# Expert values with the activations as the stationary operand, values streamed in 512 columns, and the second layer norm along the free dimension

## The chip, the core and the metric

One core of a Trainium2 chip runs the whole layer as one program. The metric is the device time of one execution in microseconds (us); the runs shown are three executions and their median.

## The reference

One layer of an encoder: 256 tokens, model width 2048. Each half is a residual sum with a gated branch and a layer norm:

```python
h = x * (1.0 + sc1) + sh1
x = layer_norm(DEEPNORM_ALPHA * x + g1 * hybrid_mixer(h, ...), ln1_g, ln1_b)
h = x * (1.0 + sc2) + sh2
x = layer_norm(DEEPNORM_ALPHA * x + g2 * peer(h, w_query, sub_keys, expert_u, expert_v), ln2_g, ln2_b)
```

`sh1 .. g2` come from `silu(c) @ W_ada + b_ada` (adaLN). `peer` picks 16 of 128 x 128 experts per head and token by product keys, takes `gelu(u . h)` of each picked expert times its softmax gate, and sums the experts' value rows with these weights:

```python
act = gelu(einsum('tkd,td->tk', u_sel, xb))
return einsum('tk,tkd->td', act * gb, v_sel)
```

## The kernel before, in words

The kernel computes the expert part densely: gates and activations of all 16384 experts for all 256 tokens, as 128 "columns" (the second key, `e2`) of 128 experts each (the first key, on the partitions). Its stages are: the input projection and the mixer; the output projection and the first layer norm; P3, the queries and the product keys; P4, gates and activations of all experts; P5, the expert values and the second layer norm. This change touches the end of the first layer norm (the residual), P3 and P5.

Arithmetic of full precision is made of matmuls on a shorter type (`fp32r`). A weight `w` is split into `hi` (a copy by ScalarE, L77) and `lo` (the rest, by VectorE, L80); an activation likewise (`split`, L118 and L119). `mm3` (L90 to L92) then adds three products to a sum: hi x hi, hi x lo and lo x hi. Weights come through `wsplit`: a load of half a megabyte on SyncE's queue (L74) into one of three `raw` tiles, then the two parts into one of three `hi` and `lo` tiles each. A few products, the "whole" ones of the input projection (L100), the score products (L736) and the transposes, take plain fp32 operands.

P5 before (L851 to L933): the sums of 16 chunks of the model dimension by 256 tokens lie in all eight PSUM banks, two chunks to a bank. A chunk's sum is 128 model columns (partitions) by 256 tokens (free). So for each expert column and each of its two halves of 1024 model columns, eight chunks follow each other: the stationary operand is a 128x128 piece of the values (`hi` or `lo`), the moving operand the 256 tokens' activations `ah` or `al`. The banks are opened beforehand by eight matmuls with a tile of zeros (L869). `GA` holds gates times activations; `a_pair` (L860) splits two columns of it at a time. It is two tiles, of FIRST = 98 and 30 columns: where the first has been used, the parts of the LAST = 6 last value columns lie (`last_column`, L874), and the end goes through these six by output chunk (L905), so that a chunk's layer norm can begin while others still grow.

Beside the values, `ada_step` (L896) loads the last part of W_ada, 16 steps of two halves, multiplies it by silu(c) on every partition (L151) and so makes `gate2`, which lies with the model dimension on the partitions (`mod[:, 5]`).

The end: gate2 and the residual `ax` (read from DRAM, written there by `residual`, L681) are put to each chunk (L916); `Norm` sums over chunks and, with a matmul by ones, over partitions; then come mean, reciprocal deviation, gain and shift (L923 to L932), and eight stores (L933). The output lies as [partition, chunk, token], and the host puts it in order.

`residual` is a generator: P3 takes two of its 16 steps per head (`next(keep)`), between the copies of the queries and the score products. The framework's scheduler, not the source's order, fixes each engine's order of instructions; weight loads carry a high priority, so they run ahead as far as free tiles allow. SyncE executes its queue in order: a load that waits for a free tile holds all that stand behind it.

Of the kernel before, what the change touches and what calls it, by code (L numbers as in the profile page):

```python
# [7 lines left out]
F32 = mybir.dt.float32  # L8
# [32 lines left out]
def layer_kernel(ctx, tc, I, out, dbg=None):  # L41
# [14 lines left out]
    ax_d = dram.tile([ND, P, S], F32, name="ax_d")  # L56
# [4 lines left out]
    iota = const.tile([P, NE], F32, name="iota")      # 0 .. 127  # L61
# [4 lines left out]
    mod = const.tile([P, 6, ND], F32, name="mod")     # shift1, 1 + scale1, gate1, shift2, 1 + scale2, gate2  # L66
    lnp = const.tile([P, 4, ND], F32, name="lnp")     # gains and shifts of the layer norms

# [1 line left out]
    def wsplit(src, pool=stream, width=1024, ahead=600, after=None):  # L70
        """A tile of weights and its two exact parts."""
# [30 lines left out]
    def proj(pss, srcs, mh, ml, nk, pool=stream, ahead_pool=None, after=None, before_last=None, beside=None, start=0):  # L102
        """pss[i][col, t] = sum over nk chunks k of srcs[i][p, k, col] * m(k)[p, t]."""
# [19 lines left out]
    def log_tables():  # L123
        """The set of tables that has both ln and exp."""
# [14 lines left out]
    def rsqrt(r, v, t):  # L139
        """One Newton step on r, which is near v ** -0.5; t is scratch."""  # L140
# [25 lines left out]
    class Norm:  # L166
        """LayerNorm of rT[p, d, t] over (d, p), chunk by chunk; s is the mean of the first chunk."""
# [12 lines left out]
        def add(self, d):  # L180
# [7 lines left out]
            else:  # L188
# [3 lines left out]
                # eps comes in once, as a share of each partition  # L192
# [5 lines left out]
        def finish(self):  # L198
            """The mean over s, and the reciprocal deviation, on every partition."""
# [21 lines left out]
    ys = [[None, None] for _ in range(32)]             # the mixer's output, in two parts  # L221
# [5 lines left out]
    scb = prm.tile([P, D], F32, name="scb")           # 2 silu(c), on every partition  # L227
# [20 lines left out]
    # dt and its sums, by token  # L248
# [17 lines left out]
    # the first half of the mixer's input as it is, for the products that take no parts  # L266
# [35 lines left out]
    def ada_input(d):  # L302
        """The mixer's input of chunk d, in two parts."""
# [12 lines left out]
    def unit_b(q, u):  # L316
        """What chunks 4q .. 4q + 3 of d add to two of the sums in SBUF."""
# [40 lines left out]
    # halves of the SSD convolution's weights: silu(u) = (u/2) (1 + tanh(u/2))  # L358
# [491 lines left out]
    with ExitStack() as p5:  # L850
# [18 lines left out]
        for b in banks:  # L869
            clear(zero, b)  # L870
# [124 lines left out]
```

## Time and profile before

| | us |
|---|---|
| median of three runs | 2599.3 (2595.35 to 2599.39) |
| span of the profiled execution | 2599.8 |
| TensorE busy in it | 2477.0 (95%) |
| VectorE busy | 1888.4 (73%) |
| ScalarE busy | 1388.1 (53%) |
| the values' matmuls, first start to last | 1844.2 to 2579.9 |

The profiled execution shows no time of its own beside its span, which lies 0.5 us above the median. Busy time of matmuls is modelled: their records overlap, so a stage is better read by counting how many of them start in a stretch of time. "PE" is the engine's matmuls, "PEld" the loads of the stationary operand, which have records of their own. A matmul on plain fp32 operands has two records.

### The profile page before, as it was taken

What the parts mean: (1) busy time and instruction counts of PE and PEld (TensorE: products, weight loads), DVE (VectorE), ACT (ScalarE), POOL (GpSimd) and SP (SyncE); (2) the same over time, 40 slices, a digit from 0 to 9 for tenths busy, and PEclk for the clock granted to TensorE, in tenths of its full rate; (3) what the DMA queues carried; (4) which work ended last, traced back from release to release, by engine and by line L of the source; (5) the groups of instructions that cost most, each with busy time, mean ns of one, the idle gap of its engine ahead of it and who ended that gap; (6) DMA issues with size and microseconds to landing.
All of it is one profiled execution on the core that took longest, in us unless ns stands there. A gap on an engine that the chain in (4) does not pass through costs nothing.

```text
span 2599.8 us, 50429 instructions
## 1 busy us (share of the span) xinstructions
PE 2477.0 (95%) x20176; PEld 2424.5 (93%) x20176; DVE 1888.4 (73%) x3281; ACT 1388.1 (53%) x2504; POOL 0.9 (0%) x7
## 2 busy tenths in 40 slices
PE   5889999999999799999999999999999999999997
PEld 5889888889999799999999999999899999999997
DVE  8788899889886899898888755555675444446545
ACT  3435576656434544499999744444334444445442
POOL 0000000000000000000000000000000000000000
PEclk9999999999999899999999999999999999999998
DMA  9887867687887665356666666666787555556651
GB/s 356 299 299 237 269 200 258 207 273 266 276 292 232 212 208 171 112 179 193 193 195 191 203 210 212 207 211 211 262 300 262 187 187 187 186 187 237 200 186 61
DMA packets 179596, 572.92 MB, mean 220 GB/s; under 512 B 20193, under 2 KB 42913, under 8 KB 179105
## 3 DMA queue, kind: packets, MB, share of 16 engines
q1 hardware_dynamic: 179362, 569.71, 66.3%
q8 instruction: 158, 2.59, 0.4%
q14 instruction: 76, 0.62, 0.1%
HBM read 556.98 MB, written 12.66 MB: 219 GB/s over the span
## 4 chain that ended last, share of the span: by engine, by line
PE 67%; DMA 15%; DVE 12%; ACT 3%; issue 2%; SPq 0%; ACTq 0%; DVEq 0%
PE ps_u L90 9%; PE ps_u L92 9%; PE ps_u L91 9%; PE ps_v L92 8%; PE ps_v L91 7%; PE ps_v L90 7%; DVE lo L80 5%; DMA adaw<-in_w_ada_dram 4%; DMA rT<-in_w_ada_dram 3%; DMA raw<-in_w_in_dram 3%; DVE adaw L151 2%; ACT hi L77 2%; DMA raw<-in_w_inB_dram 2%; PE ps_in L90 2%; PE ps_in L92 2%
## 5 line engine op out<-in xcount | busy, mean ns | idle before, releaser
L80 DVE TENSOR_TENSOR lo<-raw,hi 128x1024 fp32r<-128x1024 f32 (+1 forms) x800 | 968.7, 1213 | 522.1 <-ACT hi L77 516.3
L77 ACT ACTIVATE hi<-raw 128x1024 fp32r<-128x1024 f32 (+1 forms) x800 | 838.5, 1050 | 925.4 <-PE ps_v L91 308.9
L90 PE MATMUL ps_u<-h2h,hi 128*128 128x256 f32 x2048 | 573.2, 280 | 0.0
L92 PE MATMUL ps_u<-h2h,lo 128*128 128x256 f32 x2048 | 572.0, 279 | 0.0
L91 PE MATMUL ps_u<-h2l,hi 128*128 128x256 f32 x2048 | 571.6, 279 | 0.0
L92 PE MATMUL ps_v<-ah,lo 128*128 128x256 f32 x1952 | 548.4, 281 | 6.9 <-DVE lo L80 6.7
L90 PE MATMUL ps_v<-ah,hi 128*128 128x256 f32 x1952 | 545.4, 279 | 0.0
L91 PE MATMUL ps_v<-al,hi 128*128 128x256 f32 x1952 | 545.0, 279 | 0.0
L92 PEld LDWEIGHTS ps_u<-h2h,lo 128*128 128x128 f32 x2048 | 384.8, 188 | 0.0
L90 PEld LDWEIGHTS ps_u<-h2h,hi 128*128 128x128 f32 x2048 | 384.2, 188 | 0.0
L91 PEld LDWEIGHTS ps_u<-h2l,hi 128*128 128x128 f32 x2048 | 383.8, 187 | 0.0
L92 PEld LDWEIGHTS ps_v<-ah,lo 128*128 128x128 f32 x1952 | 366.9, 188 | 9.5 <-DVE lo L80 9.3
L91 PEld LDWEIGHTS ps_v<-al,hi 128*128 128x128 f32 x1952 | 367.5, 188 | 0.1
L90 PEld LDWEIGHTS ps_v<-ah,hi 128*128 128x128 f32 x1952 | 365.7, 187 | 0.3 <-issue 0.3
L90 PE MATMUL ps_in<-h2h,hi 128*128 128x256 f32 x768 | 223.2, 291 | 3.0 <-DVE mod L158 1.7
L92 PE MATMUL ps_in<-h2h,lo 128*128 128x256 f32 x768 | 218.4, 284 | 2.0 <-DVE lo L80 2.0
L151 DVE SCALAR_TENSOR_TENSOR adaw<-adaw,scb 128x1024 f32<-128x1024 f32 x160 | 193.6, 1222 | 34.1 <-DMA adaw<-in_w_ada_dram 33.6
L91 PE MATMUL ps_in<-h2l,hi 128*128 128x256 f32 x768 | 218.2, 284 | 0.0
L803 ACT ACTIVATE o<-eq,gT 128x128 fp32r<-128x128 f32 x512 | 160.1, 385 | 0.0
L90 PEld LDWEIGHTS ps_in<-h2h,hi 128*128 128x128 f32 x768 | 146.5, 191 | 9.2 <-issue 3.8
L92 PE MATMUL ps_o<-y,lo 128*128 128x256 f32 x512 | 145.7, 285 | 7.2 <-DVE lo L80 7.2
L92 PEld LDWEIGHTS ps_in<-h2h,lo 128*128 128x128 f32 x768 | 146.7, 191 | 4.3 <-DVE lo L80 2.2
(269 smaller groups left out, 4080.8 us busy)
## 6 DMA issues: line engine op xcount, KB each, us to landing
raw<-in_expert_u_dram SPq DMA_DIRECT2D x256, 512.0 KB, 3.8
raw<-in_expert_v_dram SPq DMA_DIRECT2D x244, 512.0 KB, 4.3
adaw<-in_w_ada_dram SPq DMA_DIRECT2D x160, 512.0 KB, 5.9
raw<-in_w_in_dram SPq DMA_DIRECT2D x110, 512.0 KB, 4.9
raw<-in_w_out_dram SPq DMA_DIRECT2D x64, 512.0 KB, 4.8
raw<-in_w_query_dram SPq DMA_DIRECT2D x64, 512.0 KB, 3.8
raw<-in_w_inB_dram SPq DMA_DIRECT2D x44, 512.0 KB, 4.4
rT<-in_w_ada_dram SPq DMA_DIRECT2D x32, 512.0 KB, 5.6
```

The lines of the kernel that those rows point to most:

```text
L77: A.activation(hi, raw, AF.Copy)
L80: V.tensor_tensor(lo, raw, hi.bitcast(F32), op=ALU.subtract)
L90: T.matmul(ps, wh, mh, start=start, stop=False)
L91: T.matmul(ps, wh, ml, start=False, stop=False)
L92: T.matmul(ps, wl, mh, start=False, stop=stop)
L151: V.scalar_tensor_tensor(w, w, 0.5, scb[:, cs], op0=ALU.mult, op1=ALU.mult, accum_out=macc[:, half, part % 2, d:d + 1])
L803: A.activation(o2[:, k], eq[:, i, 1].bitcast(F32), AF.Copy, scale=gT[:, k, t0 + i:t0 + i + 1])
```

## The change

- **Values.** A sum is now 128 tokens (partitions) by 512 model columns (free), four banks for each of two token blocks. The stationary operand is a 128x128 piece of `ah` or `al`, the moving one 512 columns of the values' parts. For a half of an expert column, eight matmuls with `hi` (two column groups, two token blocks, `ah` and `al`) come ahead of four with `lo`. The first expert column opens the banks itself; the zeros go.
- **adaLN.** A step stands behind every sixth expert column, no longer every seventh. At column 100 the sums are closed, `gate2` is written to DRAM and read back along the free dimension on every partition (`g2b`).
- **Residual.** In P3 each of the 16 chunks is transposed on TensorE (two transposes into one of the score products' two PSUM tiles), copied by ScalarE and written to DRAM by tokens.
- **End.** Four last columns, not six, go by token block and 512 columns. The layer norm's sums are taken along the free dimension as accumulators of the residual sum (VectorE) and of a square (ScalarE), per token; the gain and shift rows are loaded on every partition. The output is stored as [token, model dimension].
- FIRST goes from 98 to 66, LAST from 6 to 4. All else in the diff is comments.

```diff
-FIRST = 98         # expert columns before those that the end takes
-LAST = 6           # expert columns that the end goes through by output chunk
+FIRST = 66
+LAST = 4
...
-    def residual():
+    def residual(ps, ident):
         for d in range(ND):
             r = rT[:, d]
             V.tensor_tensor(r, r, rs, op=ALU.mult)
             A.activation(r, r, AF.Identity, scale=g1a[:, 0, d:d + 1], bias=g1a[:, 1, d:d + 1])
-            nc.sync.dma_start(ax_d[d], r)
+            pt = ps.tile([P, 2, P], F32, name="ps_r", tag="pm")
+            for tb in range(2):
+                T.transpose(pt[:, tb], r[:, tb * P:(tb + 1) * P], ident)
+            A.activation(r, pt.rearrange("p b d -> p (b d)"), AF.Copy)
+            nc.sync.dma_start(ax_d[:, :, d * P:(d + 1) * P].rearrange("b t d -> t b d"),
+                              r.rearrange("p (b d) -> p b d", b=2))
             yield
...
-        banks = [pv.tile([P, 2, S], F32, name="ps_v", tag="pm") for _ in range(8)]
-        ln = Norm(wk, pv, rT)
+        banks = [[pv.tile([P, 512], F32, name="ps_v", tag="pm") for _ in range(4)] for _ in range(2)]
+        g2b = wk.tile([P, D], F32, name="g2b")
...
-        zero = wk.tile([P, 512], BF16, name="zero5")
-        V.memset(zero, 0.0)
-        for b in banks:
-            clear(zero, b)
+        def mm_v(tb, c, ah, al, vh, vl, lo, start, stop):
+            ts = slice(tb * P, (tb + 1) * P)
+            if not lo:
+                T.matmul(banks[tb][c], ah[:, ts], vh, start=start, stop=False)
+                T.matmul(banks[tb][c], al[:, ts], vh, start=False, stop=False)
+            else:
+                T.matmul(banks[tb][c], ah[:, ts], vl, start=False, stop=stop)
...
             for half in range(2):
-                wh, wl = wsplit(I["expert_v"][e2, half])
-                for i in range(8):
-                    n = half * 8 + i
-                    mm3(banks[n // 2][:, n % 2], wh[:, i], wl[:, i], ah[:, e2 % 2], al[:, e2 % 2], False, False)
-            if e2 % 7 == 6 and e2 < 112:
-                ada_step(scb5, raw5[:2], 5, e2 // 7)
+                wh, wl = (w.rearrange("p k c -> p (k c)") for w in wsplit(I["expert_v"][e2, half]))
+                for lo in range(2):
+                    for j in range(2):
+                        js = slice(j * 512, (j + 1) * 512)
+                        for tb in range(2):
+                            mm_v(tb, 2 * half + j, ah[:, e2 % 2], al[:, e2 % 2], wh[:, js], wl[:, js], lo, e2 == 0, False)
+            if e2 % 6 == 5 and e2 < 96:
+                ada_step(scb5, raw5[:2], 5, e2 // 6)
+            if e2 == 100:
+                ada_sum(5, slice(0, ND))
+                nc.sync.dma_start(g2_d.rearrange("d p -> p d"), mod[:, 5])
+                nc.sync.dma_start(g2b, bass.AP(tensor=g2_d.tensor, offset=g2_d.offset, ap=[[0, P], [1, D]]))
...
+        def finish(tb):
...
+                ax = stream.tile([P, 1024], F32, name="ax", tag="raw", bufs=3)[:, :512]
+                nc.sync.dma_start(ax, ax_d[tb, :, c * 512:(c + 1) * 512])
+                V.tensor_tensor(r, banks[tb][c], g2b[:, c * 512:(c + 1) * 512], op=ALU.mult)
+                V.scalar_tensor_tensor(r, r, 1.0, ax, op0=ALU.mult, op1=ALU.add, accum_out=s[:, c:c + 1])
...
+                A.activation(ax, r, AF.Square, bias=sh, accum_out=s[:, 4 + c:5 + c])
...
+            for c in range(4):
+                r = rows5[tb][c]
+                V.scalar_tensor_tensor(r, r, mean, lng[c], op0=ALU.subtract, op1=ALU.mult)
+                V.scalar_tensor_tensor(r, r, rs, lnb[c], op0=ALU.mult, op1=ALU.add)
+                nc.sync.dma_start(out[tb * P:(tb + 1) * P, c * 512:(c + 1) * 512], r)
...
+        for tb in range(2):
+            fin = finish(tb)
+            next(fin)
+            for c in range(4):
+                cs = slice(c * 512, (c + 1) * 512)
+                for i in range(LAST):
+                    ah, al = as_[i // 2]
+                    for lo in range(2):
+                        mm_v(tb, c, ah[:, i % 2], al[:, i % 2], vs[i][0][:, cs], vs[i][1][:, cs], lo, False, i == LAST - 1)
+                next(fin, None)
```

In the changed kernel the two operations of `finish` on a bank are L939 and L940, its scaling L959 and L960, the load of `ax` L938, the write and the read of gate2 L914 and L915, the transposes L690, the copies behind them L691, and the values' matmuls L878, L879 and L881; other lines move by one to eight (the value loads are L75, `lo` is L81, the score products L742).

How TensorE's order begins P5 before, behind the eight zeros (out<-in, the moving operand first in each pair of names):

```order
L90 MATMUL ps_v<-ah,hi 128x256
L91 MATMUL ps_v<-al,hi 128x256
L92 MATMUL ps_v<-ah,lo 128x256
L90 MATMUL ps_v<-ah,hi 128x256
L91 MATMUL ps_v<-al,hi 128x256
L92 MATMUL ps_v<-ah,lo 128x256
```

And now, from the first matmul of P5 on:

```order
L878 MATMUL ps_v<-hi,ah 128x512
L879 MATMUL ps_v<-hi,al 128x512
L878 MATMUL ps_v<-hi,ah 128x512
L879 MATMUL ps_v<-hi,al 128x512
L878 MATMUL ps_v<-hi,ah 128x512
L879 MATMUL ps_v<-hi,al 128x512
L878 MATMUL ps_v<-hi,ah 128x512
L879 MATMUL ps_v<-hi,al 128x512
L881 MATMUL ps_v<-lo,ah 128x512 x4
```

A half column is 12 matmuls instead of 24, and `lo` is wanted behind the eighth instead of at the third.

SyncE's queue where the last half of W_ada (L162, tile rT) is loaded before (L881 is a last value column):

```order
L162 DMA rT_23081<-in_w_ada_dram 128x1024
L74 DMA raw<-in_expert_v_dram 128x1024
L881 DMA rT_23081<-in_expert_v_dram 128x1024
L74 DMA raw<-in_expert_v_dram 128x1024
L881 DMA rT_23081<-in_expert_v_dram 128x1024
```

And now (L163 is W_ada, L893 a last value column, g_d gate2 in DRAM):

```order
L163 DMA big_23146<-in_w_ada_dram 128x1024
L75 DMA raw<-in_expert_v_dram 128x1024
L893 DMA big_23146<-in_expert_v_dram 128x1024
L75 DMA raw<-in_expert_v_dram 128x1024 x2
L914 DMA g_d<-mod 128x16x1
L893 DMA big_23146<-in_expert_v_dram 128x1024
L75 DMA raw<-in_expert_v_dram 128x1024 x2
L915 DMA g2b<-g_d 128x2048
L75 DMA raw<-in_expert_v_dram 128x1024 x2
```

The write of gate2 and its reading back stand between value loads, three of those behind the last half of W_ada. Ahead of that last half the queue had 42 value loads before, and has 48 now.

The end of SyncE's queue now:

```order
L75 DMA raw<-in_expert_v_dram 128x1024 x118
L938 DMA ax<-ax_d 128x512 x3
L926 DMA lnrow<-in_ln_dram 128x1024 x4
L938 DMA ax<-ax_d 128x512 x4
L961 DMA out_dram<-big_23146 128x512 x4
L938 DMA ax<-ax_d 128x512
L961 DMA out_dram<-big_23146 128x512 x4
```

The eighth load of the residual stands behind the four stores of token block 0.

## Rows read from the trace of the kernel before

**Rows 1.** The page: span, part 1 (TensorE) and the granted clock of part 2.
```profile
span 2599.8 us, 50429 instructions
PE 2477.0 (95%) x20176; PEld 2424.5 (93%) x20176; DVE 1888.4 (73%) x3281; ACT 1388.1 (53%) x2504; POOL 0.9 (0%) x7
PEclk9999999999999899999999999999999999999998
```

**Rows 2.** Stretches of P5, the values' instructions alone: length, busy (count), clock, DMA, GB/s.
```profile
1844.20:1968.20 124.00, 117.17 (x961) 114.67 (x960) 0.00 (x0) 0.99 0.88 299
1968.20:2550.00 581.80, 581.73 (x4938) 581.41 (x4937) 0.00 (x0) 1.00 0.58 193
2550.00:2580.30 30.30, 29.99 (x252) 29.58 (x250) 6.32 (x15) 1.00 0.21 62
```

**Rows 3.** The values' matmuls of L92 (L90 and L91 alike): ns min/median/max, starts.
```profile
L92 PE MATMUL ps_v<-ah,lo x1952: 276/280/415, 1845.0 to 2545.3; 128*128 128x256 f32 x196
L92 PE MATMUL ps_v<-ah,old x96: 278/279/280, 2545.6 to 2579.9; 128*128 128x256 f32 x96
```

**Rows 4.** One stretch of 100 us inside P5, all engines, TensorE first.
```profile
2200.00:2300.00 100.00, 100.00 (x851) 100.00 (x851) 48.34 (x44) 42.55 (x45) 0.00 (x0) 1.00 0.57 186
```

**Rows 5.** Timeline of TensorE at P5's start: start us, us, what.
```profile
1845.01 0.41 PE L92 MATMUL ps_v<-ah,lo 128*128 128x256 f32 x1
...
1846.50 0.41 PE L90 MATMUL ps_v<-ah,hi 128*128 128x256 f32 x1
```

**Rows 6.** Timeline and source view of the whole products, L100.
```profile
274.46 3.62 PE L100 MATMUL ps_in<-h2w,raw 128*128 128x256 f32 x16
...
L100 PE MATMUL ps_in<-h2w,raw x224: 377/379/483, 274.5 to 570.5; 128*128 128x256 f32 x112
```

**Rows 7.** Timeline and source view of the score products, L736.
```profile
898.88 1.05 PE L736 MATMUL ps_s<-sk,qt 128*128 128x128 f32 x8
...
L736 PE MATMUL ps_s<-sk,qt x128: 270/275/377, 898.9 to 1076.1; 128*128 128x128 f32 x128
```

**Rows 8.** The loads of W_ada in P5, and all DMA from 1850 to 1950 us.
```profile
L162 SPq DMA_DIRECT2D rT<-in_w_ada_dram x32: 327/330/851, 1841.2 to 1963.2; - x32
...
DMA packets 8104, 29.50 MB, mean 295 GB/s; under 512 B 893, under 2 KB 930, under 8 KB 8097
```

**Rows 9.** DMA issues: count, KB each, median us from issue to landing.
```profile
rT<-sc_d SPq DMA_DIRECT2D x1, 1024.0 KB, 6.7
...
out_dram<-rT SPq DMA_DIRECT2D x8, 256.0 KB, 2.1
```

**Rows 10.** Timeline between P4 and P5.
```profile
1840.30 0.42 DVE L845 TENSOR_TENSOR GA<-GA,gb 128x256 f32<-128x256 f32 x1
...
1841.05 1.22 DVE L119 TENSOR_TENSOR al<-GA,ah 128x512 fp32r<-128x512 f32 x2
1841.19 1.03 PE L86 MATMUL ps_v<-zero 128*128 128x512 bf16 x2 [3.38 <-DVE zero L868]
...
1844.22 0.78 PE L90 MATMUL ps_v<-ah,hi 128*128 128x256 f32 x1
```

**Rows 11.** Timeline of the end: the last value matmul, the last operation of VectorE.
```profile
2579.87 0.28 PE L92 MATMUL ps_v<-ah,old 128*128 128x256 f32 x1
...
2595.83 0.41 DVE L932 TENSOR_SCALAR rT<-rT,lnp 128x256 f32<-128x256 f32 x1
```

**Rows 12.** Groups by line and form: busy us, mean ns of one, idle before.
```profile
L926 DVE TENSOR_TENSOR rT<-rT,ln_r 128x512 f32<-128x512 f32 x8 | 5.2, 689 | 0.0
L676 DVE SCALAR_TENSOR_TENSOR t_h<-rT,hA,ln_r 128x256 f32<-128x256 f32 x16 | 7.6, 483 | 0.0
L158 DVE TENSOR_TENSOR mod<-mod,badaT 128x1 f32<-128x1 f32 x48 | 7.5, 155 | 0.5
L118 ACT ACTIVATE ah<-GA 128x512 fp32r<-128x512 f32 x64 | 39.1, 614 | 7.5 <-PE ps_v L92 7.5
```

**Rows 13.** The same view, ScalarE's copies of the queries in P3.
```profile
L728 ACT ACTIVATE qt<-ps_q 128x256 f32<-128x256 f32 x32 | 11.7, 366 | 8.1 <-PE ps_q L92 8.1
```

More of the change, by code (lines that the diff above doesn't have):

```diff
@@ L709, in layer_kernel @@
     iota16 = iota[:, :16]
+    keep = residual(psc, ident)
     esT = [big.tile([P, 3, 8, 16], F32, name=f"es{tb}") for tb in range(2)]
@@ L852, in layer_kernel @@
         pv = pool(p5, "pv", 8, space=PSUM)
-        rT = wk.tile([P, ND, S], F32, name="rT5")
-        raw5 = [rT[:, 4 * i:4 * i + 4].rearrange("p d t -> p (d t)") for i in range(4)]
-        scb5 = rT[:, 8:].rearrange("p d t -> p (d t)")
+        big = wk.tile([P, 4, 1024], F32, name="big5")
+        raw5 = [big[:, i] for i in range(4)]
+        scb5 = big[:, 2:].rearrange("p a c -> p (a c)")
         nc.sync.dma_start(scb5, bass.AP(tensor=sc_d.tensor, offset=sc_d.offset, ap=[[0, P], [1, D]]))
-        banks = [pv.tile([P, 2, S], F32, name="ps_v", tag="pm") for _ in range(8)]
-        ln = Norm(wk, pv, rT)
+        banks = [[pv.tile([P, 512], F32, name="ps_v", tag="pm") for _ in range(4)] for _ in range(2)]
+        g2b = wk.tile([P, D], F32, name="g2b")
+        st = wk.tile([P, 2, 16], F32, name="st")
         def a_pair(e2):
@@ L904, in layer_kernel @@
         log_tables()
-        for d in range(ND):
-            cs = slice(d * P, (d + 1) * P)
-            for i in range(LAST):
-                ah, al = as_[i // 2]
-                mm3(banks[d // 2][:, d % 2], vs[i][0][:, cs], vs[i][1][:, cs], ah[:, i % 2], al[:, i % 2],
-                    False, i == LAST - 1 and d % 2 == 1)
-            if d % 2 == 0:
-                continue
-            for k in (d - 1, d):
-                ax = wk.tile([P, S], F32, name="ax", tag="ax", bufs=2)
-                nc.sync.dma_start(ax, ax_d[k])
-                V.scalar_tensor_tensor(rT[:, k], banks[k // 2][:, k % 2], mod[:, 5, k:k + 1], ax,
-                                       op0=ALU.mult, op1=ALU.add)
-                ln.add(k)
@@ L919, in layer_kernel @@
-        with tc.high_priority(offset=100):
-            dl, rs, behind = ln.finish()
-        for d in range(0, ND, 2):
-            r = rT[:, d:d + 2]
-            V.tensor_tensor(r, r, dl.unsqueeze(1).to_broadcast([P, 2, S]), op=ALU.subtract)
-        for d in range(0, ND, 2):
-            r = rT[:, d:d + 2]
-            V.tensor_tensor(r, r, rs.unsqueeze(1).to_broadcast([P, 2, S]), op=ALU.mult)
-            for k in (d, d + 1):
-                g, b = lnp[:, 2, k:k + 1], lnp[:, 3, k:k + 1]
-                if k % 4 < 3:
-                    A.activation(rT[:, k], rT[:, k], AF.Identity, scale=g, bias=b)
-                else:
-                    V.tensor_scalar(rT[:, k], rT[:, k], g, b, op0=ALU.mult, op1=ALU.add)
-            nc.sync.dma_start(out[:, d:d + 2], r)
+        lng, lnb = [], []
@@ new lines, in layer_kernel @@
+        for rows, n, tag in ((lng, 0, "hi"), (lnb, 1, "lo")):
+            for half in range(2):
+                row = stream.tile([P, 1024], F32, name="lnrow", tag=tag)
+                nc.sync.dma_start(row, bass.AP(tensor=I["ln2"].tensor, offset=I["ln2"].offset + n * D + half * 1024,
+                                               ap=[[0, P], [1, 1024]]))
+                rows += [row[:, :512], row[:, 512:]]
+        def finish(tb):
+            s = st[:, tb]
+            mean, var, rs, t0, t1, sh = (s[:, k:k + 1] for k in range(10, 16))
+            for c in range(4):
+                r = rows5[tb][c]
+                yield
+                ax = stream.tile([P, 1024], F32, name="ax", tag="raw", bufs=3)[:, :512]
+                nc.sync.dma_start(ax, ax_d[tb, :, c * 512:(c + 1) * 512])
+                V.tensor_tensor(r, banks[tb][c], g2b[:, c * 512:(c + 1) * 512], op=ALU.mult)
+                V.scalar_tensor_tensor(r, r, 1.0, ax, op0=ALU.mult, op1=ALU.add, accum_out=s[:, c:c + 1])
+                if c == 0:
+                    V.tensor_scalar(sh, s[:, 0:1], -1.0 / 512, None, op0=ALU.mult)
+                A.activation(ax, r, AF.Square, bias=sh, accum_out=s[:, 4 + c:5 + c])
+            with tc.high_priority(offset=100):
+                V.tensor_reduce(mean, s[:, 0:4], axis=AX.X, op=ALU.add)
+                V.tensor_scalar(mean, mean, 1.0 / D, None, op0=ALU.mult)
+                V.tensor_reduce(t0, s[:, 4:8], axis=AX.X, op=ALU.add)
+                V.tensor_scalar(t0, t0, 1.0 / D, EPS, op0=ALU.mult, op1=ALU.add)
+                V.tensor_tensor(t1, mean, sh, op=ALU.add)
+                V.tensor_tensor(t1, t1, t1, op=ALU.mult)
+                V.tensor_tensor(var, t0, t1, op=ALU.subtract)
+                log(rs, var)
+                A.activation(rs, rs, AF.Exp, scale=-0.5)
+                V.tensor_tensor(t0, rs, rs, op=ALU.mult)
+                V.scalar_tensor_tensor(t0, t0, -0.5, var, op0=ALU.mult, op1=ALU.mult)
+                V.scalar_tensor_tensor(rs, t0, 1.5, rs, op0=ALU.add, op1=ALU.mult)
+            for c in range(4):
+                r = rows5[tb][c]
+                V.scalar_tensor_tensor(r, r, mean, lng[c], op0=ALU.subtract, op1=ALU.mult)
+                V.scalar_tensor_tensor(r, r, rs, lnb[c], op0=ALU.mult, op1=ALU.add)
+                nc.sync.dma_start(out[tb * P:(tb + 1) * P, c * 512:(c + 1) * 512], r)
@@ new lines, in layer_kernel @@
+        rows5 = [[big[:, 2 * tb + c // 2, c % 2 * 512:c % 2 * 512 + 512] for c in range(4)] for tb in range(2)]
+        for tb in range(2):
+            fin = finish(tb)
+            next(fin)
+            for c in range(4):
+                cs = slice(c * 512, (c + 1) * 512)
[4 more added lines that the diff above has]
+                next(fin, None)
@@ L968, in _layout @@
     r["w_out"] = n["w_out"][0].reshape(32, P, ND, P).transpose(2, 1, 0, 3).reshape(ND, P, 32 * P)
-    r["lnp"] = np.stack([cols(n[k][0]) for k in ("ln1_g", "ln1_b", "ln2_g", "ln2_b")], axis=1)
+    r["lnp"] = np.stack([cols(n[k][0]) for k in ("ln1_g", "ln1_b")], axis=1)
+    r["ln2"] = np.stack([n["ln2_g"][0], n["ln2_b"][0]])
     r["w_query"] = n["w_query"][0].reshape(ND, P, 32, P).transpose(2, 1, 0, 3).reshape(32, P, D)
@@ L988 @@
         args[name] = nc.dram_tensor(f"in_{name}_dram", a.shape, _mybir.dt.from_np(a.dtype), kind="ExternalInput").ap()
-    out = nc.dram_tensor("out_0_dram", (P, ND, S), F32, kind="ExternalOutput").ap()
+    out = nc.dram_tensor("out_0_dram", (S, D), F32, kind="ExternalOutput").ap()
     with _tile.TileContext(nc) as tc:
@@ L992 @@
     r = _run(nc, [arrays], core_ids=[0])
[L993 to L994 removed]
+    return r.results[0]["out_0_dram"].reshape(1, S, D)
```

9 lines of the change are left out of this document (3 added, 6 removed).

## The prediction

> **What bounds the kernel now.** I read the page first: TensorE is busy for 95% of the span at nearly full granted clock [rows 1]. Since matmul ends are modelled, busy says little, so I next counted matmuls by stretch. The expert values run from 1844.2 to 2580.3 us, and the middle 582 us of them is one unbroken stream without a stall worth naming [rows 2]; it holds 3 x (1952 + 96) = 6144 matmuls of 256 columns [rows 3]. Inside it, 851 start in 100 us: **117.5 ns each** [rows 4]. 256 columns at 2.4 GHz take 106.7 ns, so 10.8 ns per matmul is something else. What that something is decides the case, and three views speak on it.
>
> - At P5's start, behind an idle 3.38 us [rows 10], the clock is at its lower level, 1.2 GHz. There seven matmuls take 1.49 us, 213 ns each [rows 5], which is 256 columns and nothing more. So the 10.8 ns isn't a charge that every matmul pays; it shows only where streaming is short.
> - The input projection's whole products are recorded as passes: 16 starts in 3.62 us, the last lasting 0.38, so (3.62 - 0.38)/15 = 216 ns a pass [rows 6]. That is 512 columns' worth at 2.4 GHz (213.3) plus 2.7 ns. Each pass has a weight load of its own, and the load hides.
> - So a pass of a whole product takes its columns twice. By that measure the score products, of 128 columns, stream 106.7 ns like the values' matmuls; their loads are as wide, and they start every (1.05 - 0.275)/7 = 111 ns [rows 7].
>
> I read this as a floor of 111 to 117 ns from one weight load to the next, which a stream of 213 ns covers. The Trainium skill, in TensorE: Matmul & The Clock Gate, section Back-to-back issue gap, gives 262 cycles (109 ns) for 256 columns and 518 (216 ns) for 512. The values' spacing [rows 4] disagrees with the first, the passes [rows 6] agree with the second; by the page alone the saving would be 8 us, not the one below.
>
> **The change part by part**, against the profiled span of 2599.8 us (the runs' median is 0.5 us lower).
>
> *The stream.* 6144 matmuls of 256 columns become 3072 of 512, so the columns stay and half the weight loads go. At 117.5 ns the old ones take 721.9 us; at 216 ns the new ones take 663.6. **-58 us.** The two other readings of the 10.8 ns are rivals A and B.
>
> *adaLN beside the values.* The gate's 32 loads of w_ada sit at the stage's start, from 1841.2 to 1963.2 [rows 8]. Over 1844.2 to 1968.2 the DMA engines moved 299 GB/s, and TensorE started 961 matmuls where 124 us hold 1055 [rows 2]: this stretch is bound by DMA. SyncE's order now puts 48 value halves rather than 42 ahead of the last w_ada half, so 80 halves rather than 74 come in: 122 x 80/74 = 132 us at the same rate. Forty-eight halves would need 48 x 12 x 0.216 = 124.4 us of TensorE, so 7.5 us is lost where 122 - 42 x 24 x 0.1175 = 3.6 was lost before. **+4**, from 0 (the wider spacing feeds better) to +10.
>
> *gate2 along the free dimension.* gate2 goes to DRAM as 128x16 single elements and comes back on every partition. SyncE stops at the read until the write has landed, and the value loads queue behind, just where the buffers are drained. The trace has no such write. From below it is an ordinary landing of 2.1 us [rows 9], hidden. From above, 2048 packets at the 8104 in 100 us of that stretch [rows 8] take 25 us. I take 10: the bytes (8 KB) are nearest to the small landing, the count is not. With 3.5 us for the 1 MB read at 299 GB/s (one such took 6.7 alone [rows 9]), less some 3.5 halves of 2.6 us in the buffers: **+5**, from 0 to +20. The Trainium skill, DMA: Bandwidth & Descriptors, section Rules for kernel authors, speaks against this edit: a last dimension that isn't contiguous costs a descriptor per element. No row here shows one.
>
> *The stage's start.* Eight bank-clearing matmuls go, which waited for a memset and kept the first product until 1844.22 [rows 10]. The new first products need `al`, ready about 1.4 us behind GA L845 at 1840.3, so 2.8 us earlier; but TensorE idles as long before, and the stretch runs at 1.2 GHz, where 2.8 us is worth half. **-1.5**, from -4 to 0.
>
> *The end.* Before, 19.6 us lie between the last matmul at 2579.87 + 0.28 and the end of the span [rows 11]. Now token block 0 is normalised beside the matmuls of block 1. Behind the last matmul: L939 0.69, two L940 at 0.75, the square 0.63, nine operations on one column at 0.16, eight 128x512 scaling operations at 0.75 and a store of 2.1 [rows 9, 12]; with 0.6 for logarithm and exponential on ScalarE that is 13. (0.75 lies between 0.69, a plain 128x512 operation, and 0.97, twice the 0.483 of a 256 one with a per-partition scalar.) The eighth residual load queues behind four stores of block 0: +1.5. 14.5 for 19.6: **-5**, from -9 to 0.
>
> *The residual in P3.* Thirty-two transposes at 111 ns [rows 7] are 3.6 us on TensorE. The score tiles share two PSUM places with the transposes, so the scores wait for two ScalarE copies of 0.37 [rows 13] behind six to ten other matmuls (0.7 to 1.2 us of cover): I add 0.2 a head. **+5**, from +2 to +9 if a weight copy gets in between. The residual's other steps run in the first heads, as before.
>
> *At nothing:* the gates' boundary of 66 instead of 98 columns (256 elements per token pair in two instructions either way) and four last columns instead of six, hidden under the stream; without that cover each half costs a copy and a subtraction, 2.3 us.
>
> **Sum:** -58 + 4 + 5 - 1.5 - 5 + 5 = -50.5, so 2549.3 for the profile and **2549** for the median. The forecast's own range is 2536 (both DMA terms at 0, the end at -9) to 2564 (the write of gate2 at +20).
>
> **The rivals.**
>
> *A: part of the 10.8 ns stays with every matmul* (224 ns for 512). The spacing of today allows it [rows 4]; the passes speak against [rows 6]. The stream gives 721.9 - 3072 x 0.224 = 34 instead of 58: **2573**.
>
> *B: the moving operand is read at 256 columns in 117.5 ns*, 2.18 per ns, and 512 need 235. For it: no row shows the values' kind of matmul reading faster, as the whole products' passes may read 256 columns once for two turns [rows 6]. Against it: the score products read half as many and are still at 111 [rows 7]. The stream gives nothing, the other terms but the w_ada one +3.5: **2603**, no change.
>
> *C, the slower side: the weight load comes out from under the stream.* The stationary operand is now `ah` and `al` alternating over two token blocks, in the same array that streams 512 columns. If a quarter of the 111 ns between loads [rows 7] stuck out, a matmul would take 216 + 28 = 244 ns, the stream 749.6, and the sum would be 2599 + 27.7 + 3.5 = **2630**. It decides where the stream gives less than the 3.5, from 234 ns on, 18 ns exposed. Against it: behind the whole products' passes loads of that width hide [rows 6]. The Trainium skill has a harsher form (TensorE: Matmul & The Clock Gate, Part 3, The mechanism): loads overlap running matmuls only where row groups differ, and here all use all rows. By that rule, a pair would take 213 + 111 = 324 ns, and the stream 273 us more than now. The trace disagrees: 117.5 ns [rows 4] is far less than 106.7 + 111.
>
> That the change does not do what it says is out: TensorE's order shows 3072 matmuls of 128x512.
>
> **How the numbers follow.** The forecast gets 0.71, A 0.15, B 0.08, C 0.06. A measurement of this kernel can tell about 0.2%, 5.2 us. Forecast and A are faster, B is the same, C slower; a tenth of B's chance goes to slower, where the write of gate2 is dear: 0.86, 0.07, 0.07. The range runs from 2536 to 2577, which takes in A and leaves out B, C and the forecast's own corners.
>
> **What would show it.** Between w_ada's last load and the end, matmuls of 512 columns start every 216 ns (463 in 100 us): 224 is A, 235 B, more C. The scores in P3 show waits for ScalarE under 0.5 us. TensorE shows one wait of about 5 us on L81 where g2b is read. From the last matmul to the end are 13 to 16 us. A spacing of over 226 ns, or over 20 us of idle TensorE between 1845 and 2000 us, would make the forecast wrong.

## The result, and the profile after

The change takes 2551.9 us (median of four, 2550.3 to 2557.1) against 2597.6 for the kernel before on the same chip: ratio 0.983, 95% interval 0.982 to 0.985. The profiled execution took 2552.6 us, its span is 2550.7. The forecast was 2549. One of the ten executions of run e4, further below, took 8487 us and is left out of its figures. By stages, though, the time came from other places than the forecast said. From the first matmul of each stage in the two traces, in us (a sum's tile names its stage: ps_in the input projection, ps_o the output projection, ps_q the queries of P3, ps_u the activations of P4, ps_v the values of P5):

| stretch | before | after | difference |
|---|---|---|---|
| start to the first query matmul (P3) | 866.9 | 862.9 | -4.0 |
| P3, to the first ps_u | 209.2 | 208.7 | -0.5 |
| P4, ps_u's first start to last end | 761.7 | 744.1 | **-17.6** |
| from there to P5's first product | 6.4 | 1.8 | -4.6 |
| P5, first product to last end | 735.9 | 719.5 | **-16.4** |
| the end | 19.6 | 13.7 | -5.9 |

The largest gain is in P4, whose own code the diff leaves alone but for one constant, FIRST. The page after, as in [rows 1]:

```profile
span 2550.7 us, 44290 instructions
PE 2424.6 (95%) x17122; PEld 2248.3 (88%) x17122; DVE 1862.2 (73%) x3255; ACT 1381.3 (54%) x2506; POOL 0.9 (0%) x7
```

TensorE's share is the same, so one has to count again. The next view gives, by stretch: its length, TensorE's busy time (count of matmuls), granted clock, DMA share, GB/s. The count takes in the two or three matmuls that were already running. The changed kernel, in P4 (256 columns), in P5 at the adaLN loads and the g2 transfers, and in P5's middle:

```profile
1500.00:1800.00 300.00, 300.00 (x2650) 1.00 0.68 218
1900.00:1950.00 50.00, 49.22 (x214) 1.00 0.91 319
1950.00:1960.00 10.00, 10.00 (x45) 1.00 0.73 209
1960.00:1980.00 20.00, 11.92 (x44) 0.83 0.70 240
1980.00:2000.00 20.00, 20.00 (x89) 1.00 0.78 259
2050.00:2300.00 250.00, 250.00 (x1094) 1.00 0.61 200
```

And the kernel before in P4 and in P5's middle:

```profile
1500.00:1800.00 300.00, 300.00 (x2550) 1.00 0.66 210
2050.00:2300.00 250.00, 250.00 (x2125) 1.00 0.57 186
```

- P4's matmuls of 256 columns, the same instructions in the same order, start every 300/2647.5 = **113.3 ns** instead of 300/2547.5 = **117.8**.
- P5's matmuls of 512 columns start every 250/1092 = **228.9 ns**; the forecast had 216. Its own 463 in 100 us are 438 here.
- Around the g2 transfers 44 matmuls stand in 20 us, 89 in the next 20: 45 x 0.2289 = 10.3 us lost, with the granted clock down to 0.83.

TensorE's waits in P5 and the transfers from 1945 to 1985 us in the changed kernel (first the engine, line <- what ended the wait: us, times, longest; then packets, and issues with count, KB each, us to landing):

```profile
PE ps_v L878 <- ACT hi L78: 8.1, 2, 5.6
PE ps_v L878 <- ACT ah L119: 1.8, 1, 1.8
```
```profile
DMA packets 4638, 9.92 MB, mean 248 GB/s; under 512 B 2350, under 2 KB 2350, under 8 KB 4508
g_d<-mod SPq DMA_DIRECT2D x1, 8.0 KB, 12.1
```

The write of 8 KB has 2048 elements, and of the packets in this stretch 2350 are under 512 bytes; it lands after 12.1 us. The Trainium skill's rule that the prediction cited (DMA: Bandwidth & Descriptors, Rules for kernel authors: a last dimension that is not contiguous is one descriptor per element) agrees with this packet count.

The end, where [rows 11] show it before: last value matmul and the last scaling operations.

```profile
2536.55 0.40 PE L881 MATMUL ps_v<-old,ah 128*128 128x512 f32 x1
2544.26 2.74 DVE L960 SCALAR_TENSOR_TENSOR big<-big,st,lnrow 128x512 f32<-128x512 f32 x4
```

### The profile page after: what moved, and what is told of

It is laid out like the page before. It is cut to its first block, busy times and chain, and to the rows that moved or that the text cites. A ratio compares the mean times of both kernels' runs of the same rounds, so it can differ in the third digit from the quotient of the medians.

```text
span 2550.7 us, 44290 instructions
## 1 busy us (share of the span) xinstructions
PE 2424.6 (95%) x17122; PEld 2248.3 (88%) x17122; DVE 1862.2 (73%) x3255; ACT 1381.3 (54%) x2506; POOL 0.9 (0%) x7
## 4 chain that ended last, share of the span: by engine, by line
PE 67%; DMA 15%; DVE 12%; ACT 3%; issue 2%; SPq 1%; DVEq 0%; ACTq 0%
PE ps_u L91 9%; PE ps_u L92 9%; PE ps_u L93 9%; PE ps_v L879 8%; PE ps_v L881 8%; PE ps_v L878 8%; DVE lo L81 5%; DMA adaw<-in_w_ada_dram 4%; DMA raw<-in_w_in_dram 3%; DMA big<-in_w_ada_dram 2%; ACT hi L78 2%; DVE adaw L152 2%; DMA raw<-in_w_inA_dram 2%; PE ps_q L93 2%; PE ps_q L92 2%
## 5 line engine op out<-in xcount | busy, mean ns | idle before, releaser
L81 DVE TENSOR_TENSOR lo<-raw,hi 128x1024 fp32r<-128x1024 f32 (+1 forms) x804 | 972.1, 1212 | 506.8 <-ACT hi L78 504.7
L78 ACT ACTIVATE hi<-raw 128x1024 fp32r<-128x1024 f32 (+1 forms) x804 | 843.6, 1051 | 884.6 <-PE ps_v L879 302.1
L91 PE MATMUL ps_u<-h2h,hi 128*128 128x256 f32 x2048 | 568.7, 278 | 0.0
L92 PE MATMUL ps_u<-h2l,hi 128*128 128x256 f32 x2048 | 568.1, 277 | 0.0
L878 PE MATMUL ps_v<-hi,ah 128*128 128x512 f32 x992 | 390.1, 393 | 9.9 <-ACT hi L78 8.1
L879 PE MATMUL ps_v<-hi,al 128*128 128x512 f32 x992 | 390.7, 394 | 1.2 <-DVE al L120 1.2
L91 PEld LDWEIGHTS ps_u<-h2h,hi 128*128 128x128 f32 x2048 | 386.2, 189 | 0.0
L92 PEld LDWEIGHTS ps_u<-h2l,hi 128*128 128x128 f32 x2048 | 384.6, 188 | 0.0
L881 PE MATMUL ps_v<-lo,ah 128*128 128x512 f32 x992 | 268.9, 393 | 0.8 <-DVE lo L81 0.8
L878 PEld LDWEIGHTS ps_v<-hi,ah 128*128 128x128 f32 x992 | 187.5, 189 | 52.3 <-ACT hi L78 8.9
L879 PEld LDWEIGHTS ps_v<-hi,al 128*128 128x128 f32 x992 | 187.7, 189 | 43.0 <-DVE al L120 1.6
L91 PE MATMUL ps_in<-h2h,hi 128*128 128x256 f32 x768 | 222.3, 289 | 3.0 <-DVE mod L159 2.2
L881 PEld LDWEIGHTS ps_v<-lo,ah 128*128 128x128 f32 x992 | 186.8, 189 | 42.0 <-DVE lo L81 2.0
L92 PE MATMUL ps_in<-h2l,hi 128*128 128x256 f32 x768 | 217.6, 283 | 0.0
L91 PEld LDWEIGHTS ps_in<-h2h,hi 128*128 128x128 f32 x768 | 146.6, 191 | 9.0 <-issue 4.2
```

The lines of the kernel that those rows point to most:

```text
L78: A.activation(hi, raw, AF.Copy)
L81: V.tensor_tensor(lo, raw, hi.bitcast(F32), op=ALU.subtract)
L878: T.matmul(banks[tb][c], ah[:, ts], vh, start=start, stop=False)
L879: T.matmul(banks[tb][c], al[:, ts], vh, start=False, stop=False)
L881: T.matmul(banks[tb][c], ah[:, ts], vl, start=False, stop=stop)
```

## The experiments

**Where tiles start.** Why should unchanged matmuls go faster? One line of the change that the section on it left out shortens a tile at the bottom of SBUF, so every tile above it on the left, the weights' parts among them, starts 128 bytes lower in each partition; h2h, h2l, ah and al lie on the right and stay. Where each tile starts stands in the built programs, not in the traces. I call "difference" the start of the moving operand less that of the stationary one, modulo 256 bytes. It is 64 in all large groups of the kernel before. In the changed kernel it is 192 for h2h and h2l against the weights (ps_in, ps_q, ps_u), 64 for ps_o, which goes at 117.8 ns in both traces but for short stretches, and 64 for the values.

```diff
-    lnp = const.tile([P, 4, ND], F32, name="lnp")
+    lnp = const.tile([P, 2, ND], F32, name="lnp")
```

Run e1: this alone, on the kernel before.

```diff
     (the kernel before)
-    lnp = const.tile([P, 4, ND], F32, name="lnp")
+    lnp = const.tile([P, 2, ND], F32, name="lnp")
...
+        lnp2 = wk.tile([P, 4, ND], F32, name="lnp2")
+        nc.sync.dma_start(lnp2[:, 0:2], I["lnp"][:, 2:4])
...
```

> The kernel before with one thing of the change alone: the constant tile of layer norm gains is 128 bytes per partition shorter (the second norm's rows are loaded in P5 instead), so every tile on the left of SBUF, the weights among them, starts 128 bytes lower, while h2h, h2l, ah and al stay. No matmul, order or size changes. Theory 'places' (the spacing of matmuls hangs on where stationary and moving tile start, modulo 256 bytes: 64 apart in every stage that goes at 117.8 ns, 192 apart where 113.3 shows): ps_u comes down from 117.8 to 113.3 for most of its 6144 matmuls, as in the changed kernel, and ps_v with it, so P4 is about 20 us shorter and P5 up to 27: 2550 to 2578 us. Theory 'order' (P4 became faster through something else that the change brought, such as the gates' boundary at 66 columns or the way in which the stage is entered): 117.8 ns everywhere, 2597 within 5 us.

Measured: 2557.6 us (2544.5 to 2575.5), ratio 0.987 (0.981 to 0.993); profiled span 2546.8. The same two stretches in e1:

```profile
1500.00:1800.00 300.00, 300.00 (x2650) 1.00 0.69 218
2050.00:2300.00 250.00, 250.00 (x2208) 1.00 0.59 194
```

113.3 ns in P4 and in P5. In this trace P4 takes 742.2 us and P5 709.9, so the kernel before with 128 bytes less is as fast in P4 as the changed kernel and 9.6 us faster in P5. "Order" is out, and with it the gates' boundary, which e1 leaves at 98.

Run e2: the changed kernel with the 128 bytes put back. Run e3: the changed kernel with the values' operands moved against each other instead. Run e4: with 64 bytes.

```diff
     (e2; e4 has P, 16)
+    gap = const.tile([P, 32], F32, name="gap")
+    V.memset(gap, 0.0)
```
```diff
     (e3, the last tile of P5's pool on the right)
+        wk.tile([P, 32], F32, name="gap5")
```

> The changed kernel with the 128 bytes put back as an unused tile behind the layer norm gains. 'Places': ps_u is 64 apart again and goes back to 117.8 ns, so P3 and P4 are about 20 us longer; ps_v of 512 columns is 192 apart now and falls from 229 towards 220 to 224, so P5 is 15 to 27 us shorter: 2540 to 2560 us, but with the time in another stage. 'Order': ps_u stays at 113.3 and ps_v at 229, 2552 within 5 us. A third theory, that 229 is what 512 columns cost wherever they lie: ps_u at 117.8, ps_v at 229, 2572.

> The changed kernel with an unused 128 bytes in P5's pool on the right, so that ah and al start 128 bytes lower and the values' matmuls have their operands 192 apart; all else stays. 'Places': ps_u stays mostly at 113.3, ps_v falls from 229 to 220 to 224: 2525 to 2537 us, faster than both kernels. 229 wherever they lie, or 'order': 2552 within 5 us.

> The changed kernel with an unused 64 bytes behind the layer norm gains: h2h against the weights, and the values against ah and al, are both 128 apart modulo 256. 'Places': both spacings move, to where no run has shown yet; if what counts is nearness (modulo 256) to 64, they lie between the two levels or at the lower one. 'Order': 113.3 and 229 as in the changed kernel, 2552 within 5 us.

Measured: e2 2582.8 us (2576.6 to 2584.8), ratio 0.995 (0.993 to 0.997); e3 2563.1 (2560.4 to 2572.4), ratio 0.988 (0.985 to 0.992); e4 2585.8 (2582.2 to 2593.2), ratio 0.998 (0.996 to 1.000). Their stretches, e2, e3 and e4 in this order:

```profile
1500.00:1800.00 300.00, 300.00 (x2550) 1.00 0.65 210
2050.00:2300.00 250.00, 250.00 (x1073) 1.00 0.60 196
```
```profile
1500.00:1800.00 300.00, 300.00 (x2650) 1.00 0.68 218
2050.00:2300.00 250.00, 250.00 (x1073) 1.00 0.60 196
```
```profile
1500.00:1800.00 300.00, 300.00 (x2530) 1.00 0.65 209
2050.00:2300.00 250.00, 250.00 (x1078) 1.00 0.61 197
```

P4 obeys: 117.8 ns in e2, 113.3 in e3, 118.7 in e4. P5 went against the expectation: at a difference of 192, good for 256 columns, 512 columns take 250/1071.5 = 233.3 ns, more than at 64. So e2 and e3 are slower than expected. That places matter holds, and that 192 is good for both sizes falls.

Runs e5 and e6: is it the difference, or a start off some boundary? Unused tiles in the pools move all operands to multiples of 64 bytes, e5 with the differences of the changed kernel (and 192 for ps_o), e6 with a difference of 0.

```diff
-    lnp = const.tile([P, 2, ND], F32, name="lnp")
+    const.tile([P, 24], F32, name="gap")
...
+    lnp = prm.tile([P, 2, ND], F32, name="lnp")
...
+    h2p.tile([P, 8], F32, name="gap_r")
...
+        wk.tile([P, 8], F32, name="gap5")
```

(e6 has 8 instead of 24, and a gap of 16 ahead of lnp.)

> The changed kernel with all operands moved so that they start at multiples of 64 bytes (they start at 32 modulo 64 in every run so far), and with the differences of the changed kernel kept: h2h 192 behind the weights, ah and al 192 behind the values, and ps_o's y now 192 behind the weights as well. Theory 'difference alone': ps_u 113.3 and ps_v 228.9 as in the changed kernel, ps_o down from 117.8 towards 113.3 (1536 x 4.45 ns = up to 7 us): 2545 to 2552 us. Theory 'boundary' (a start off the 64-byte grid costs reads, and this is what is left over 106.7 ns per 256 columns): both spacings fall, ps_u towards 107 to 110 and ps_v to 213 to 218, 2480 to 2520 us.

> As the run before, but with a difference of 0: all operands start at 192 modulo 256. 'Difference alone' has no row for 0; the four differences tried gave 117.8 (64), 118.7 (128) and 113.3 (192) for 256 columns, so 0 lies from 113 to 119 and ps_v from 228.9 to 233.3: 2545 to 2590 us. 'Boundary': ps_u 107 to 110, ps_v 213 to 218.

Measured: e5 2551.6 us (2547.0 to 2562.6), e6 2584.9 (2581.9 to 2589.7), ratios 0.985 (0.981 to 0.989) and 0.998 (0.996 to 1.001). The stretches, e5 first:

```profile
1500.00:1800.00 300.00, 300.00 (x2650) 1.00 0.68 218
2050.00:2300.00 250.00, 250.00 (x1094) 1.00 0.61 200
```
```profile
1500.00:1800.00 300.00, 300.00 (x2502) 1.00 0.64 206
2050.00:2300.00 250.00, 250.00 (x1105) 1.00 0.62 202
```

e5 repeats the changed kernel's counts to the last matmul, with other absolute starts: "boundary" falls, and the difference predicts the spacing. (It is no full account: one difference can have two levels, as the last section shows.) At 0, 256 columns are at their slowest, 120.0 ns, and 512 at their fastest, 250/1103 = 226.7.

Runs e9 and e10: two more differences for each size, by gaps as above (e9: 24 in the place of lnp, no others; e10: 8 behind lnp and 32 in P5's pool).

> The changed kernel with other differences (start of the moving operand less that of the stationary one, modulo 256): 224 for h2h against the weights, 192 for y against the weights, 32 for the values against ah and al. By the rows so far 256 columns take 120.0 ns at 0, 117.8 at 64, 118.7 at 128, 113.3 at 192; 512 columns 226.7 at 0, 228.9 at 64, 232.4 at 128, 233.3 at 192. Theory 'difference alone, smooth in steps of 32': ps_u lies between its values at 192 and 0 (113.3 to 120), ps_v between those at 0 and 64 (226.7 to 228.9), ps_o goes to 113.3. If what counts is the 64-byte step alone, ps_u is 113.3 or 120.0 and ps_v 226.7 or 228.9, nothing between.

> The same for 160 (h2h against the weights) and 224 (values against ah and al). 'Smooth in steps of 32': ps_u between 113.3 and 118.7, ps_v between 226.7 and 233.3; by the 64-byte step alone, one of the two ends of each.

The stretches, e9 first:

```profile
1500.00:1800.00 300.00, 300.00 (x2538) 1.00 0.65 209
2050.00:2300.00 250.00, 250.00 (x1073) 1.00 0.61 197
```
```profile
1500.00:1800.00 300.00, 300.00 (x2560) 1.00 0.66 211
2050.00:2300.00 250.00, 250.00 (x1073) 1.00 0.61 196
```

2583.3 and 2584.7 us, one execution each. Neither form of the theory holds. For 256 columns 160 and 224 give 117.3 and 118.3 ns, between their neighbours but far from 113.3. For 512 columns 32 gives 233.3, slower than both its neighbours, and 224 gives 233.3 too. Of the places tried, 256 columns have one good one; 512 columns have one too, and 64 comes next. All together, ns per matmul in the middle of P4 and of P5, where nothing interrupts the stream:

| difference, bytes | 0 | 32 | 64 | 128 | 160 | 192 | 224 |
|---|---|---|---|---|---|---|---|
| 256 columns | 120.0 | | 117.8 | 118.7 | 117.3 | **113.3** | 118.3 |
| 512 columns | **226.7** | 233.3 | 228.9 | 232.3 | | 233.3 | 233.3 |

The two rows differ in more than the columns. With 256 the weights, on the left of SBUF, are the stationary operand; with 512 they are the moving one. No run separates the size from this exchange.

A rival is the traffic of VectorE and ScalarE, which write and read the same tiles. The traces speak against it: between two starts with both engines idle P4's spacing is 117.8 ns before and 113.5 after, between two with both at work 117.8 and 113.6.

**Is it bytes or matmuls?** e1 and e6 together say that half the weight loads buy nothing: 6144 x 113.3 and 3072 x 226.7 ns, each at its best place tried, are both 696 us. Run e7 halves the bytes, by another type.

```diff
-            ah = wk.tile([P, 2, S], F32R, name="ah", tag="ah", bufs=3)
+            ah = wk.tile([P, 4, S], BF16, name="ah", tag="ah", bufs=3)[:, :2]
...
+            hi = stream.tile([P, 2048], BF16, name="hi", tag="hi")[:, :1024]
...
```

> The changed kernel with ah, al and the values' hi and lo in bf16: the same matmuls of 512 columns at the same places, each operand half the bytes. (The products are of less precise parts, otherwise nothing is left out.) Theory 'moving read' (TensorE gets its fp32r columns at 115.6 ns per 256, the middle of the two levels, whatever the number of weight loads): with half the bytes the spacing falls from 228.9 to the columns' own 213.3, at most 216, and P5 is 3072 x 13 to 15 ns = 40 to 47 us shorter: 2505 to 2512 us. Theory 'per matmul' (a fixed 15 ns between one matmul and the next): 228.9 stays, 2552.

Measured: 2526.3 us, one execution. The timeline of TensorE in e7 (start us, us, what), two neighbouring half columns:

```profile
2201.52 0.38 PE L889 MATMUL ps_v<-hi,ah 128*128 128x512 bf16 x1
...
2204.11 0.38 PE L889 MATMUL ps_v<-hi,ah 128*128 128x512 bf16 x1
```

Twelve matmuls in 2.59 us are 216 ns each, the value that the prediction had read off the fp32 passes. "Per matmul" falls: what lies above the columns' 213.3 hangs on the operands' type. That it is the bytes is argued, as the type changes with them. The Trainium skill gives 518 cycles, 216 ns, for 512 columns (TensorE: Matmul & The Clock Gate, section Back-to-back issue gap): bf16 agrees here, fp32r took 226.7 to 233.3. The run changes both operands, and its weight loads are recorded at 98 ns instead of 188, so whether the excess sits in reading the moving one, the stationary one or both together isn't separated. P5 is 686.0 us, 33.5 less than in the changed kernel, where 3072 x 13 = 40 was expected: TensorE now catches up with VectorE and the loads, and waits 20.2 us in P5 (9.4 on hi, 7.2 on lo, 3.6 on al) against 11.9. The total fell by 26 only, as P5 began 6.5 us later in this execution.

**The write of g2.** Run e8 takes the two transfers off SyncE.

```diff
-                nc.sync.dma_start(g2_d.rearrange("d p -> p d"), mod[:, 5])
-                nc.sync.dma_start(g2b, ...)
+                G.dma_start(g2_d.rearrange("d p -> p d"), mod[:, 5])
+                G.dma_start(g2b, ...)
```

> The changed kernel with the write of g2 to DRAM and its read back issued by POOL, which is idle, rather than SyncE. Theory 'SyncE stops' (the value loads queue behind the read, which waits for the write's landing): the two waits on the values' first copy, 8.1 us, and the lower clock behind them go, 2541 to 2546 us. Theory 'queue of packets' (2048 single elements hold up the value loads on the DMA engines themselves): the wait stays, 2552 within 4 us.

Measured: 2549.5 us (2545.9 to 2552.9), ratio 0.983 (0.980 to 0.986), as the changed kernel. Its stretches, and the write's landing:

```profile
1960.00:1965.00 5.00, 4.37 (x20) 1.00 1.17 163
1965.00:1970.00 5.00, 0.00 (x0) 0.70 0.95 97
```
```profile
g_d<-mod POOLq DMA_DIRECT2D x1, 8.0 KB, 14.3
```

SyncE is free and has issued value loads up to 1961.0 us, yet the DMA engines are as good as full while they move 97 to 163 GB/s. The single elements fill them: "queue of packets".

Run e11 writes g2 one chunk of d at a time, and puts the values at a difference of 0 (the gaps of e5, with 56 instead of 8 in P5's pool); run e12 has the same places, but VectorE turns g2 in blocks of 32x32 first.

```diff
     (e11; the read stands at e2 == 116)
...
+            if 97 <= e2 < 97 + ND:
+                d = e2 - 97
+                nc.sync.dma_start(g2_d[d:d + 1].rearrange("d p -> p d"), mod[:, 5, d:d + 1])
```
```diff
     (e12)
...
-                nc.sync.dma_start(g2_d.rearrange("d p -> p d"), mod[:, 5])
+                V.tensor_copy(g2p[:, :ND], mod[:, 5])
+                V.transpose(g2t, g2p)
+                for b in range(4):
+                    nc.sync.dma_start(g2_d[:, 32 * b:32 * b + 32], g2t[32 * b:32 * b + ND])
```

> The changed kernel with three things put together: all 256-column groups at a difference of 192 and the values at 0 (226.7 ns, 3072 x 2.2 = 7 us less); and g2 written to DRAM one chunk of d at a time, over 16 expert columns behind the adaLN loads, and read back behind them, so that no transfer of 2048 single elements stands between value loads that the DMA engines are late with. The waits on the values' first copy near 1965 us (8.1 us, and the lower clock behind them) should go, 10 us by the 45 matmuls that are missing there: 2530 to 2540 us. If the single elements cost the value loads as much when spread, the 10 us stay: 2542 to 2548.

> The places of the run before (256-column groups at 192, values at 0), with g2 turned in 32x32 blocks by VectorE ahead of its write, so that the write is 64 runs of 32 elements rather than 2048 single ones; write and read stand where the changed kernel has them. Theory 'single elements' (their 2048 packets take the DMA engines some 10 us in which the value loads come late): the write lands in 2 to 4 us, the waits on the values' first copy fall from 12.4 us in the run before, 8.1 in the changed kernel, to under 3, and nothing between 1950 and 2000 us runs at the lower clock: 2528 to 2538 us. Theory 'the read' (the 1 MB read of g2b behind the drained buffers is what costs): the waits stay at 5 us or more, 2538 to 2550.

Measured: e11 2551.3 us (2540.8 to 2553.7), ratio 0.983 (0.981 to 0.986); **e12 2526.9 us** (2525.1 to 2535.6), ratio 0.975 (0.973 to 0.977). P5's middle has the same count in both, 226.7 ns as planned. The landing of e11's writes, and its wait on hi in P5:

```profile
g_d<-mod SPq DMA_DIRECT2D x16, 0.5 KB, 10.5
```
```profile
PE ps_v L880 <- ACT hi L78: 12.4, 5, 4.3
```

For e12 the transfers, all of TensorE's waits in P5, and two stretches:

```profile
g2b<-g_d SPq DMA_DIRECT2D x1, 1024.0 KB, 7.3
g_d<-g2t SPq DMA_DIRECT2D x4, 2.0 KB, 2.9
```
```profile
PE ps_v L882 <- ACT ah L119: 1.8, 1, 1.8
PE ps_v L883 <- DVE al L120: 1.2, 1, 1.2
PE ps_v L885 <- DVE lo L81: 1.0, 3, 0.4
```
```profile
1950.00:2000.00 50.00, 50.00 (x223) 1.00 0.80 268
2050.00:2300.00 250.00, 250.00 (x1105) 1.00 0.63 202
```

Spreading fails, and the time is above both expectations: the sixteen writes were all issued between 1942.6 and 1971.1 us, still among value loads that came late, and waits grew to 12.4 us. With 64 runs of 32 elements the write lands in 2.9 us, no wait on hi is left, and TensorE runs through the stretch where the changed kernel lost 10.3 us. The 1 MB read stands where it stood, with its 7.3 us, so "the read" is out. e12 beats both kernels; it takes about 1% less than the changed one.

## Why the prediction came out, and where it was wrong

The number held and its largest reason did not. Its terms, against the traces:

| term | forecast | measured |
|---|---|---|
| the stream | -58 | -20.5 |
| adaLN loads and g2 in P5 | +4 and +5 | about -8 and +10 |
| the stage's start | -1.5 | -4.6 + 3.0 = -1.6 |
| the end | -5 | -5.9 |
| P3 with the residual | +5 | -0.5 |
| P4 | 0 | -17.6 |
| before P3 | 0 | -4.0 |

- **The stream: the step that failed** is "at 216 ns the new ones take 663.6". The passes of [rows 6] do take 216 ns, but they are no measure for fp32r. The text itself gave the reason under B, that they may read 256 columns once for two turns, and gave it 0.08. At 228.9 ns the stream is 3072 x 0.2289 = 703.2 us, 20.5 less than 723.6. By spacing A had 224 and B 235, so the truth lies between the rivals; the text's own bound for being wrong, "A spacing of over 226 ns", is passed. B's mechanism is the nearest: the excess goes with the operands' type (e7), and halving the loads gave nothing at the best places (e1, e6), so the text's floor of 111 to 117 ns from one weight load to the next, which a longer stream covers, isn't there. The 512 columns gained only because the values before lay at a difference of 64 and went at 117.8; against 113.3, 6144 of which are 696.1 us, they would have lost 7.
- **P4 at nothing** was the second failed step. "All else in the diff is comments" overlooked the tile that shrank. 128 bytes gave the 17.6 us in P4: alone they take it from 761.7 to 742.2 us (e1), and put back, from 744.1 to 763.6 (e2). The stream fell short by 37.5 us. P4 made up for nearly half of that, the adaLN loads for about 12, P3 for 5.5 and the part before it for 4.0. That these came to about as much as the stream lacked is luck.
- **adaLN.** The 299 GB/s of [rows 2] was read as the DMA engines' ceiling. The changed kernel moved 319 from 1900 to 1950 and has 214 matmuls there where an undisturbed 50 us have 220; that is 1.4 us lost. The kernel before lost 10.7 by [rows 2] (961 of 1052 at 117.8 ns), of which 1.3 belong to the start; the text had reckoned with 3.6. So the sign was wrong: about -8 for +4.
- **g2.** The size, 5 in a range up to 20, is 10.3 measured. Of the mechanism, the single elements were right, and e12 shows that they are all of it; SyncE's stop, by which the text reckoned, costs nothing more (e8). The wait that it looked for on L81 came on L78, the values' first copy.
- **Start.** The first product comes 4.6 us earlier and waits 1.8 us for ah. But the first 10 us of P5 go at the lower clock for longer than before. The view of all matmuls, before first:

```profile
1844.20:1854.20 10.00, 10.00 (x75) 0.87 0.75 254
1817.50:1827.50 10.00, 8.77 (x25) 0.66 0.83 289
```

One of the 75 is a bank-clearing matmul. 74 start where 85 fit and 25 where 44 fit, which is 1.3 and 4.3 us lost (1.2 of the 4.3 is a wait for al). What is left of the 4.6 is 1.6, as worked out.
- **End.** The 13.7 us lie in the 13 to 16 named.
- **P3.** The forecast wanted waits under 0.5 us on ScalarE; there are three on the transposes' copy, 5.4 us in all, longest 3.0. The query matmuls run faster (431 and 432 in 50 us from 950 and 1000 us, 423 and 424 before; 1149 of 1536 ps_q start 112 to 115 ns apart), which is worth up to 5.1 us. But e1, which has this without the transposes, gains only 1.2 in P3 (208.0 us), as its score products wait 7.6 us for the copies of the queries, 2.7 before. So at like places the residual costs less than the +5 of the sum: 0.7 us against e1 (208.7), 2.2 with the 128 bytes put back (e2, 211.4 against 209.2, a quarter of its query matmuls at the faster level). Each is from one profile.
- **Before P3** the 4.0 us can't be told from scatter: the other profiles at a difference of 192 have 850.7 to 866.3 us there, with the same matmuls.
- **C, the slower side,** decided from 234 ns on; the slowest place has 233.3, just short of it. Whether any of that is load time, e7 leaves open, as said.

## What to carry to other kernels

Compare the spacing of the instructions that a change leaves alone, too: a tile that shrinks moves all that lies above it, and here the places of two operands were worth as much as the rewriting (17.6 us in P4, 16.4 in P5). Before rewriting a stream of fp32r matmuls for fewer weight loads, try a few unused bytes between the operands' pools. Turn a column into rows on an engine before it goes to DRAM: single elements fill the DMA engines even when no queue waits for them.

## What was not expected of the hardware

- The spacing of fp32r matmuls has good places, modulo 256 bytes (table above), and they differ for the two forms of 256 and 512 columns. Why stays open, and not every step of 32 was tried. For 512 columns at 0 nothing speaks for a modulus of 512: the operands lie 256 apart modulo 512 in e6 and 0 in e12, and both have 226.7 ns.
- At 192 the 256-column stream has two levels, 113.3 and 117.8 ns, and an interruption can switch it; at 64 it has the same two. In P4's first half of the changed kernel the gates' pairs stand behind every 24 ps_u:

```profile
1201.90 0.40 PE L814 MATMUL ps_g<-o,eq 128*128 128x256 f32 x2
...
1204.87 0.39 PE L814 MATMUL ps_g<-o,eq 128*128 128x256 f32 x2
...
1207.92 0.40 PE L814 MATMUL ps_g<-o,eq 128*128 128x256 f32 x2
```

The 24 between the first two start 113 to 114 ns apart in the trace, those between the next two 117 to 119, and so on in turn. At 64, ps_o in the kernel before and in e1, the same instructions at the same difference:

```profile
802.00:850.00 48.00, 48.00 (x410) 1.00 0.68 210
802.00:850.00 48.00, 48.00 (x426) 1.00 0.69 211
```

Over the last 477 matmuls of this product that is 117.8 ns before and 113.3 in e1. So a difference makes one level likely and doesn't bar the other. Where P4 has no gates, the stream stayed at 113.3 in all eight profiles at 192 and at 117.8 in both at 64, and the times go with it: e3 and e2 have the values at the same spacing and h2h at 192 and 64, and their executions lie apart, 2560.4 to 2572.4 and 2576.6 to 2584.8 us. What picks the level at an interruption is open. It may be why e1's executions spread over 31 us, and those of the kernel before, over all runs here, from 2569 to 2600; no run tried to choose the level.
